# A value bank copied to SBUF, a SiLU issued two products later, four products held in their order

## The chip, the core and the metric

The kernel runs on one core of a Trainium2 chip. The metric is device time in microseconds (us) for one execution. TensorE (PE in the rows; PEld is its weight load), VectorE (DVE), ScalarE (ACT), GpSimd (POOL) and the DMA queue of SyncE (SP) each work through an instruction stream of their own in order and wait for each other by semaphores.

## The reference

One layer of a diffusion backbone over 1024 tokens of width 1024: a token mixer, and then a ConvGLU channel mixer, which is where the change lies. With `D_FF = 2816` and tokens on a grid of 16 rows by 64:

```python
p = h @ w_up_l                            # 1024 -> 2 * 2816
val, gate = p[..., :D_FF], p[..., D_FF:]
gate = depthwise_3x3(gate on the grid)    # one 3x3 filter per channel
out = (silu(gate) * val) @ w_down_l       # 2816 -> 1024
```

Everything is float32.

## The kernel before

Each float32 product is made of three matmuls on rounded high and low parts (`mm3`, lines 189 to 193: high by high, high by low, low by high). The channels of the up projection are handled in 22 blocks `f` of 128 channels. The tokens are in two groups of 512, so a block has four results: gate for group 0 and 1, value for group 0 and 1.

**Blocks 0 and 1** are made plainly. `pvs[f][0]` and `pvs[f][1]` are the gates, `pvs[f][2]` and `pvs[f][3]` the values, each 128x512 in one PSUM bank. There are eight banks of that size: two under the tag `mm`, three under `g`, one under `a`, and a pair `cv`. The loop over `d` (lines 1691 to 1702) finishes `pvs[f][1]` and `pvs[f][3]` with `up2` while the second token group is still being turned, and `sums` builds the token operands for what follows.

**Blocks 2 to 21** take seven products each in place of eight (a Strassen-Winograd scheme over the halves of the input channels and the two column groups). A product is 12 matmuls of 128x128 by 128x512. I write f.p for product p of block f; the order traced in `seq` is 2.1, 2.2, 2.5, 2.6, 2.3, 2.7, 3.1, 2.4, 3.5, 3.2, 3.6, 3.3, 3.7, 4.1, 3.4, 4.5, 4.2 and so on. They accumulate in three banks of a block: A (tag `g`) takes products 1, 6, 7 and 4, B (tag `mm`) product 2, C (tag `mm`) products 5 and 3. After products 1, 5, 6 and 7 the bank is copied to SBUF by ScalarE (line 1734), and the next product into that bank waits for the copy. A is let go by the value multiply of its own block; B and C by the writes into `pad` (lines 1741 and 1745).

**Behind the products** runs `finish(f)`: nine taps of the 3x3 filter over `pads[f % 2]` into `cv` (the first on ScalarE, line 1489, eight on VectorE, line 1491), then the SiLU of `cv` (ScalarE, line 1495), then two multiplies by the value (`mul`, VectorE, recorded at line 1468 like every sum of `tt`) and a store. `cv` is one buffer, so a block's taps start when the SiLU before is done, and `pads` are two, so the writes into the pad of block f wait for the taps of block f-2. These steps stand in a queue `back`, from which `work` takes two or three after each product.

When the products of block 2 start, `pvs[1][2]` has been copied to SBUF (`spare`, line 1576), and its `g` bank goes to A of block 2. The other two `g` banks hold `pvs[0][3]` and `pvs[1][3]`, until the second multiplies of blocks 0 and 1. A of block 3 takes the first of them, A of block 4 the second.

Pages (`pg`) are 36 SBUF buffers of 128x1024 that token operands, weights, gates and split parts share.

The framework's planner orders the instructions of each engine: it steps through the traced program with costs of its own and issues what it thinks is ready, earlier traced first. So the order on an engine is that of the plan, and where the chip is slower than the plan somewhere, an engine waits in that order. `tc.issue_after(x)` ties what is traced in its block behind `x` on the same engine, in the order of issue only.

Of the kernel before, what the change touches and what calls it, by code (L numbers as in the profile page):

```python
# [12 lines left out]
AF = mybir.ActivationFunctionType  # L13
# [5 lines left out]
P = 128  # L19
# [25 lines left out]
def grp(ap, g):  # L45

    v = ap.rearrange("p (a n) -> p a n", a=4)
    return v[:, 1:3] if g == 0 else v[:, 0::3]
# [52 lines left out]
class Kern:  # L101
# [87 lines left out]
    def mm3(self, out, ah, al, bh, bl, start, stop, **kw):  # L189
        nc = self.nc  # L190
        nc.tensor.matmul(out, ah, bh, start=start, stop=False, **kw)  # L191
        nc.tensor.matmul(out, ah, bl, start=False, stop=False, **kw)  # L192
        nc.tensor.matmul(out, al, bh, start=False, stop=stop, **kw)  # L193

    def rsqrt(self, out, ss, scale, pool):

# [1248 lines left out]
    def ffn(self):  # L1445
        nc, tc, A = self.nc, self.tc, self.A
        V = nc.vector
        wu = A["w_up"][0].rearrange("(k p) n -> p k n", p=P)
        with tc.tile_pool(name="ffn", bufs=1, reuse_waits="tile") as fp:
# [5 lines left out]
            g = [None] * NF  # L1455
# [11 lines left out]
            def tt(eng, o, a, b, op=ALU.add):  # L1467
                eng.tensor_tensor(o, a, b, op=op)  # L1468
# [3 lines left out]
            back = deque()  # L1472
            convd = set()

            def work(n):
                for _ in range(n):
                    if back:
                        back.popleft()()

            def finish(f, val):  # L1480

                c3 = self.cv.rearrange("p (r c) -> p r c", c=64)
                pad = pads[f % 2]

                def tap(k):
                    w = self.dw[:, k * NF + f:k * NF + f + 1]
                    src = pad[:, k // 3:k // 3 + 16, k % 3:k % 3 + 64]
                    if k == 0:
                        nc.scalar.mul(c3, src, w)  # L1489
                    else:  # L1490
                        V.scalar_tensor_tensor(c3, src, w, c3, op0=ALU.mult, op1=ALU.add)  # L1491

                def silu():
                    g[f] = self.pg()
                    nc.scalar.activation(g[f], self.cv, AF.Silu)

                def mul(i):
                    gt = g[f]
                    tt(V, grp(gt, i), grp(gt, i), val(i).rearrange("p (a n) -> p a n", a=2), ALU.mult)
                    if i and f < NF - 5:  # L1500
                        nc.sync.dma_start(gd[f], gt)
                        g[f] = None

                for k in range(9):
                    back.append(lambda k=k: tap(k))
                back.append(lambda: convd.add(f))
                back.append(silu)
                back.append(lambda: mul(0))
                back.append(lambda: mul(1))
# [14 lines left out]
            def to_pad(f, j, pv):  # L1524
                for rows, c in (((5, 13), 0),) if j == 0 else (((1, 5), 0), ((13, 17), 256)):
                    n = rows[1] - rows[0]
                    nc.scalar.copy(pads[f][:, rows[0]:rows[1], 1:65],
                                   pv[:, c:c + 64 * n].rearrange("p (r c) -> p r c", c=64))
# [37 lines left out]
            pvs = [[None] * 4 for _ in range(2)]  # L1566
# [8 lines left out]
                        turn(0)  # L1575
            nc.scalar.copy(self.spare, pvs[1][2])
            pvs[1][2] = self.spare

# [12 lines left out]
            def gpart(f, i):  # L1593

                if f not in here:
                    here[f] = [f >= NF - 5] * 2
                    if not here[f][0]:
                        g[f] = self.pg()
                c = slice(512 * i, 512 * i + 512)
                if not here[f][i]:  # L1600
                    nc.sync.dma_start(g[f][:, c], gd[f][:, c])
                    here[f][i] = True
                return g[f][:, c]
# [38 lines left out]
            def load(f):  # L1642
                if f >= NF or f in raws:
                    return
                raws[f] = []
                for col in (DFF + f * P, f * P):
                    if f % 2:
                        r = self.pg().rearrange("p (k n) -> p k n", k=ND)
                    else:
                        r = self.wp.tile([P, ND, P], F32, tag="raw", bufs=2, name=self.nm("wr"))  # L1650
                    nc.sync.dma_start(r, wu[:, :, col:col + P])
                    raws[f] += [flat(r[:, 0:4]), flat(r[:, 4:8])]

            def prepw(f, p, paged=False):
                a00, a01, a10, a11 = raws[f]
                S = Ss.setdefault(f, {})
                e = (V, nc.gpsimd)
                if p in (1, 2, 4):
                    src = {1: a00, 2: a01, 4: a11}[p]
                else:  # L1660
                    src = S[p] = big("s")
                    a, b = {5: (a10, a11), 6: (S.get(5), a00), 3: (a01, S.get(6)), 7: (a00, a10)}[p]
                    tt(e[(8 if f > 9 else 160) >> p & 1], src, a, b, ALU.add if p == 5 else ALU.subtract)
                if paged:
                    hl = self.page2()
                    h, l = hl[:, 0], hl[:, 1]
                else:
                    h = self.wp.tile([P, 512], F32R, tag="wh", bufs=4, name=self.nm("wh"))
                    l = self.wp.tile([P, 512], F32R, tag="wl", bufs=4, name=self.nm("wl"))
                nc.scalar.copy(h, src)  # L1670
                self.sub_l(nc.gpsimd, l, src, h)
                W[f, p] = h, l
# [11 lines left out]
            B = {1: h0[:4], 2: h0[4:], 3: h1[4:], 4: TB[3], 5: TB[0], 6: TB[1], 7: TB[2]}  # L1684
# [21 lines left out]
                    sums(d)  # L1706
            for f in range(2):
                to_pad(f, 1, pvs[f][1])
            for f in range(2):
                finish(f, lambda i, f=f: pvs[f][2 + i])  # L1710

# [2 lines left out]
            for n, (f, p) in enumerate(seq):  # L1714
                if n + WA < len(seq):
                    f2, p2 = seq[n + WA]
                    load(f2)
                    if p2 == 1:
                        load(f2 + 1)
                    prepw(f2, p2)  # L1720
                x = st.setdefault(f, {})
                bank = {2: "B", 5: "C", 3: "C"}.get(p, "A")
                if p in (1, 2, 5):
                    x[bank] = self.psum({"A": "g", "B": "mm", "C": "mm"}[bank])
                ps = x[bank]
                h, l = W.pop((f, p))
                for d in range(4):
                    c = slice(d * P, d * P + P)
                    b = B[p][d]
                    self.mm3(ps, h[:, c], l[:, c], b[:, 0], b[:, 1], start=(d == 0 and p in (1, 2, 5)), stop=(d == 3),  # L1730
                             skip_group_check=True)
                if p in (1, 5, 6, 7):
                    x[p] = big("m")
                    nc.scalar.copy(x[p], ps)
                pad = pads[f % 2]
                if p == (6 if f == 2 else 2):

                    while f - 2 not in convd:
                        work(1)
                    r = lambda t: t.rearrange("p (r c) -> p r c", c=64)  # L1740
                    tt(V, pad[:, 5:13, 1:65], r(x["B"]), r(x[1]))
                if p == 3:
                    for o, c in ((1, 0), (13, 256)):
                        r = lambda t: t[:, c:c + 256].rearrange("p (r c) -> p r c", c=64)
                        tt(V, pad[:, o:o + 4, 1:65], r(ps), r(x[6]))
                    finish(f, lambda i, x=x: (x["A"], x[5])[i])
                if p == 7:
                    tt(nc.gpsimd, x[5], x[5], x[7])
                work(2 + (len(back) > 14))
                if n >= len(seq) - 7:  # L1750
                    for _ in range(3):
                        if order:
                            gpart(order.pop(0), 0)
                if n >= len(seq) - 4:
                    i = len(ops)
                    ops[i] = prep(i)
# [49 lines left out]
            for ps in range(7):  # L1806
                bk = banks[BSET[ps]]
                for j in range(NJ):
                    n = ps * NJ + j
# [82 lines left out]
```

## Time and profile before

| what | us |
|---|---|
| three timed executions | 1362.15, 1360.96, 1357.66 |
| their median | 1360.96 |
| the profiled execution | 1357.89 |
| its span, first to last instruction | 1356.1 |

The profiled execution lies 3.07 us under the median and 1.79 us above its own span. Times in the rows are from the start of the span. The first 700 us are the mixer; products of blocks 2 to 21 run from about 733 to 1120, the down projection after that. A small share of the matmul records is missing from the trace.

### The profile page before, as it was taken

Reading aid. Unit: us, or ns where it says so; the run is one execution under the profiler, and the core shown is the slowest. Engines: PE = TensorE matmul, PEld = TensorE weight load, DVE = VectorE, ACT = ScalarE, POOL = GpSimd, SP = SyncE. Lnnn points to the kernel's source line nnn. Section 1 sums busy time; section 2 is a strip of 40 time slices with the busy share of each in tenths; the row PEclk is TensorE's granted clock in tenths of the full one; section 3 lists DMA queues with packets and bytes.
Section 4 is the critical chain, followed back from the end, with each engine's and each line's share of the span. In section 5 each row is a group of like instructions: output and inputs, shape, how many; then the busy total and the mean of one; then the engine's idle time right before and its main releaser. Section 6 shows DMA issues by size and latency. Waiting matters only on the chain.

```text
span 1356.1 us, 19253 instructions
## 1 busy us (share of the span) xinstructions
PE 1282.6 (95%) x6678; PEld 1023.2 (75%) x6678; DVE 987.9 (73%) x1750; ACT 636.5 (47%) x1324; POOL 472.2 (35%) x464
## 2 busy tenths in 40 slices
PE   5999999999899999999999899999999999999994
PEld 3777886567557789887777688888888887888883
DVE  4465555944973856757369899878888789878997
ACT  4663456532554233444757444444444444555442
POOL 0220114332434252542125667666665650000000
PEclk9999999999999999999999999999999999999997
DMA  9622226676476877815432233331233156645665
GB/s 341 196 85 72 73 84 198 210 212 210 154 202 235 270 235 273 281 61 171 171 124 79 78 93 94 94 93 60 67 93 94 47 192 235 215 127 173 200 226 187
DMA packets 183731, 213.67 MB, mean 158 GB/s; under 512 B 31639, under 2 KB 119761, under 8 KB 183633
## 3 DMA queue, kind: packets, MB, share of 16 engines
q1 hardware_dynamic: 181553, 208.19, 47.8%
q0 software_dynamic: 864, 3.15, 0.7%
q8 instruction: 53, 0.87, 0.3%
q10 hardware_dynamic: 1216, 1.09, 0.2%
q14 instruction: 45, 0.37, 0.1%
HBM read 163.11 MB, written 49.28 MB: 157 GB/s over the span
## 4 chain that ended last, share of the span: by engine, by line
PE 45%; DVE 16%; issue 5%; DMA 4%; ACT 4%; POOL 3%; SPq 0%; DVEq 0%; POOLq 0%; ACTq 0%
PE ps L191 12%; PE ps L193 11%; PE ps L192 11%; PE ps L1098 4%; DVE cv L1491 3%; PE ps L1042 2%; DVE pg L1468 1%; POOL pg L165 1%; DVE s L1468 1%; PE ps L312 1%; POOL pg L1023 1%; DVE pg L165 1%; DVE wl L165 1%; DVE pad L1632 1%; PE ps L1029 1%
## 5 line engine op out<-in xcount | busy, mean ns | idle before, releaser
L191 PE MATMUL ps<-pg,wh 128*128 128x512 f32 (+1 forms) x896 | 351.3, 393 | 7.7 <-DVE pad L1468 5.5
L193 PE MATMUL ps<-pg,wl 128*128 128x512 f32 (+1 forms) x896 | 346.5, 387 | 0.0
L192 PE MATMUL ps<-pg,wh 128*128 128x512 f32 (+1 forms) x896 | 345.9, 386 | 0.0
L1491 DVE SCALAR_TENSOR_TENSOR cv<-pad,dw,cv 128x1024 f32<-128x1024 f32 x176 | 226.3, 1286 | 12.0 <-ACT cv L1489 8.6
L191 PEld LDWEIGHTS ps<-pg,wh 128*128 128x128 f32 x896 | 169.8, 190 | 55.9 <-issue 21.0
L193 PEld LDWEIGHTS ps<-pg,wl 128*128 128x128 f32 x896 | 169.7, 189 | 35.8 <-issue 3.5
L192 PEld LDWEIGHTS ps<-pg,wh 128*128 128x128 f32 x896 | 169.9, 190 | 30.4 <-issue 0.4
L165 POOL TENSOR_TENSOR wl<-wr,wh 128x512 fp32r<-128x512 f32 x68 | 89.8, 1327 | 185.5 <-ACT wh L183 157.4
L165 POOL TENSOR_TENSOR wl<-s,wh 128x512 fp32r<-128x512 f32 x80 | 107.2, 1342 | 61.6 <-ACT wh L1670 61.3
L1670 ACT CAST wh<-s 128x512 fp32r<-128x512 f32 x80 | 49.5, 622 | 119.4 <-PE ps L192 116.5
L193 PE MATMUL ps<-wh,pg 128*128 128x512 f32 x250 | 98.1, 394 | 2.6 <-POOL pg L165 2.6
L191 PE MATMUL ps<-wh,pg 128*128 128x512 f32 x250 | 97.9, 393 | 2.2 <-ACT pg L1635 1.7
L192 PE MATMUL ps<-pg,pg 128*128 128x512 f32 (+1 forms) x248 | 96.8, 392 | 3.0 <-POOL pg L165 2.8
L191 PE MATMUL ps<-pg,pg 128*128 128x512 f32 (+1 forms) x248 | 98.1, 397 | 1.1 <-DVE pg L493 0.8
L192 PE MATMUL ps<-wl,pg 128*128 128x512 f32 x250 | 97.4, 390 | 0.0
L193 PE MATMUL ps<-pg,pg 128*128 128x512 f32 (+1 forms) x248 | 95.9, 391 | 0.8 <-POOL pg L165 0.6
L1098 PE MATMUL ps<-pg,pg 128*128 128x128 f32 x464 | 59.0, 277 | 0.9 <-ACT pg L1158 0.9
L1098 PEld LDWEIGHTS ps<-pg,pg 128*128 128x128 f32 x464 | 55.4, 192 | 3.2 <-ACT pg L1158 1.2
L192 PEld LDWEIGHTS ps<-pg,pg 128*128 128x128 f32 x248 | 47.3, 191 | 13.4 <-POOL pg L165 3.6
L193 PEld LDWEIGHTS ps<-wh,pg 128*128 128x128 f32 x250 | 47.1, 188 | 13.1 <-POOL pg L165 3.5
L191 PEld LDWEIGHTS ps<-pg,pg 128*128 128x128 f32 x248 | 47.3, 191 | 12.4 <-DVE pg L493 1.2
L193 PEld LDWEIGHTS ps<-pg,pg 128*128 128x128 f32 x248 | 46.9, 190 | 12.6 <-issue 1.7
(364 smaller groups left out, 2419.2 us busy)
## 6 DMA issues: line engine op xcount, KB each, us to landing
pg<-in_w_down_dram SPq DMA_DIRECT2D x97, 256.0 KB, 4.2
wr<-in_w_ada_dram SPq DMA_DIRECT2D x32, 512.0 KB, 4.8
wr<-in_w_up_dram SPq DMA_DIRECT2D x24, 512.0 KB, 4.1
wr<-in_w_in_dram SPq DMA_DIRECT2D x20, 512.0 KB, 3.8
pg<-in_w_up_dram SPq DMA_DIRECT2D x20, 512.0 KB, 6.5
wr<-in_w_down_dram SPq DMA_DIRECT2D x35, 256.0 KB, 2.9
gd<-pg SPq DMA_DIRECT2D x17, 512.0 KB, 2.9
pg<-gd SPq DMA_DIRECT2D x34, 256.0 KB, 4.0
```

The source lines that it names most:

```text
L165: eng.tensor_tensor(l, full, h.bitcast(F32), op=ALU.subtract)
L191: nc.tensor.matmul(out, ah, bh, start=start, stop=False, **kw)
L192: nc.tensor.matmul(out, ah, bl, start=False, stop=False, **kw)
L193: nc.tensor.matmul(out, al, bh, start=False, stop=stop, **kw)
L312: nc.tensor.matmul(ps[32 * j:32 * j + 32, :], self.csil[:, k, :], t[:, a, :], start=(k < 4), stop=(k >= 4), skip_group_check=True, tile_po ...
L1023: nc.gpsimd.tensor_tensor(dst[:, d].rearrange("p h (b c) -> p h b c", b=4), src.unsqueeze(2).broadcast_to([P, H, 4, 32]), mask, op=ALU.mult)
L1029: nc.tensor.matmul(ps[:, h * P:(h + 1) * P], Wt[:, d, h], Q[:, d, h], start=True, stop=True, skip_group_check=True)
L1042: nc.tensor.matmul(ps[po, h * n:(h + 1) * n], Q[k0:k0 + kn, d, h, po], R[k0:k0 + kn, d, h, c0:c0 + n], start=True, stop=True, skip_group_c ...
L1098: nc.tensor.matmul(ps[:, hs(h)], lhs(h), rhs(h), start=True, stop=True, skip_group_check=True)
L1468: eng.tensor_tensor(o, a, b, op=op)
L1491: V.scalar_tensor_tensor(c3, src, w, c3, op0=ALU.mult, op1=ALU.add)
L1670: nc.scalar.copy(h, src)
```

## The change

`pvs[0][3]`, a value of block 0, is copied by ScalarE to half a page as soon as it is complete, and the multiply reads the copy. Six empty steps ahead of the SiLU of block 0 in `back` have it traced after product 2.7 and its copy, two products later than before. The SiLUs of blocks 0 and 1 are tied behind the newest product copy on ScalarE. Products 6 to 9 of `seq` (3.1, 2.4, 3.5, 3.2) are each tied behind the last matmul traced before them.

```diff
@@ mm3
-        nc.tensor.matmul(out, al, bh, start=False, stop=stop, **kw)
+        self.lastmm = nc.tensor.matmul(out, al, bh, start=False, stop=stop, **kw)
@@ finish
                 def silu():
                     g[f] = self.pg()
-                    nc.scalar.activation(g[f], self.cv, AF.Silu)
+                    with tc.issue_after(self.copied.ins) if f < 2 else ExitStack():
+                        nc.scalar.activation(g[f], self.cv, AF.Silu)
...
                 back.append(lambda: convd.add(f))
+                if f == 0:
+
+                    back.extend([lambda: None] * 6)
                 back.append(silu)
@@ ffn
             pvs[1][2] = self.spare
+            spare2 = self.pg()[:, 0:512]
...
                 to_pad(f, 1, pvs[f][1])
+            nc.scalar.copy(spare2, pvs[0][3])
+            pvs[0][3] = spare2
...
-                for d in range(4):
-                    c = slice(d * P, d * P + P)
-                    b = B[p][d]
-                    self.mm3(ps, h[:, c], l[:, c], b[:, 0], b[:, 1], start=(d == 0 and p in (1, 2, 5)), stop=(d == 3),
-                             skip_group_check=True)
+                with tc.issue_after(self.lastmm.ins) if 6 <= n < 10 else ExitStack():
+                    for d in range(4):
+                        c = slice(d * P, d * P + P)
+                        b = B[p][d]
+                        self.mm3(ps, h[:, c], l[:, c], b[:, 0], b[:, 1], start=(d == 0 and p in (1, 2, 5)), stop=(d == 3),
+                                 skip_group_check=True)
                 if p in (1, 5, 6, 7):
                     x[p] = big("m")
-                    nc.scalar.copy(x[p], ps)
+                    self.copied = nc.scalar.copy(x[p], ps)
```

## Rows read from the trace of the kernel before

**Rows 1.** The head of the page.

```profile
span 1356.1 us, 19253 instructions
```

**Rows 2.** Busy time by stretch: engine busy us (instructions), granted clock, DMA share, GB/s.

```profile
750.00:757.00 7.00, 1.69 (x8) 1.07 (x6) 6.73 (x7) 1.49 (x2) 3.44 (x3) 0.99 0.26 75
...
760.00:850.00 90.00, 90.00 (x398) 74.49 (x397) 81.49 (x81) 38.83 (x61) 60.22 (x46) 1.00 0.31 93
850.00:1100.00 250.00, 249.51 (x1100) 206.04 (x1099) 204.64 (x210) 110.44 (x173) 157.87 (x119) 1.00 0.27 80
...
1150.00:1300.00 150.00, 150.00 (x664) 124.24 (x663) 132.70 (x214) 75.52 (x139) 0.00 (x0) 1.00 0.58 190
1300.00:1356.00 56.00, 37.51 (x161) 29.59 (x159) 48.57 (x120) 19.54 (x44) 0.00 (x0) 0.86 0.54 191
```

**Rows 3.** PE's waits from 700 us on: total us, times, longest us.

```profile
PE ps L191 <- DVE pad L1468: 5.5, 1, 5.5
...
PE ps L191 <- ACT pg L1635: 1.7, 1, 1.7
```

**Rows 4.** PE in order of time around the stall: start, us, instruction [idle before].

```profile
743.21 0.50 PE L191 MATMUL ps<-pg,wh 128*128 128x512 f32 x1 [1.24 <-ACT m L1734]
...
751.30 0.39 PE L193 MATMUL ps<-pg,wl 128*128 128x512 f32 x1
757.22 0.76 PE L191 MATMUL ps<-pg,wh 128*128 128x512 f32 x1 [5.54 <-DVE pad L1468]
```

**Rows 5.** VectorE in order of time, 749 to 776 us.

```profile
749.67 6.58 DVE L1491 SCALAR_TENSOR_TENSOR cv<-pad,dw,cv 128x1024 f32<-128x1024 f32 x5
756.38 1.36 DVE L1468 TENSOR_TENSOR pad<-ps,m 128x512 f32<-128x512 f32 x3
757.65 1.27 DVE L1468 TENSOR_TENSOR pg<-pg,ps 128x512 f32<-128x512 f32 x2
...
765.41 0.69 DVE L1468 TENSOR_TENSOR s<-s,wr 128x512 f32<-128x512 f32 x1 [2.63 <-POOL wl L165]
...
774.27 0.70 DVE L1468 TENSOR_TENSOR pg<-pg,spare 128x512 f32<-128x512 f32 x1 [0.30 <-ACT pg L1495]
774.89 0.67 DVE L1468 TENSOR_TENSOR pg<-pg,ps 128x512 f32<-128x512 f32 x1
```

**Rows 6.** ScalarE in order of time, 738 to 758 us.

```profile
738.36 0.62 ACT L1463 CAST pg<-m 128x512 fp32r<-128x512 f32 x1 [4.57 <-DVE m L1468]
...
740.46 1.16 ACT L1489 ACTIVATE cv<-pad,dw 128x1024 f32<-128x1024 f32 x1
...
756.28 1.02 ACT L1495 ACTIVATE pg<-cv 128x1024 f32<-128x1024 f32 x1 [5.51 <-DVE cv L1491]
757.21 0.58 ACT L1734 COPY m<-ps 128x512 f32<-128x512 f32 x1
```

**Rows 7.** Line 1576, the copy to spare: ns min/median/max.

```profile
L1576 ACT COPY spare<-ps x1: 577/577/577, 707.7 to 707.7; 128x512 f32<-128x512 f32 x1
```

**Rows 8.** Busy time by stretch after the stall (columns as rows 2).

```profile
757.20:760.50 3.30, 3.28 (x8) 2.62 (x9) 3.26 (x6) 2.14 (x4) 2.37 (x2) 0.52 0.22 82
757.20:777.80 20.60, 20.58 (x84) 16.92 (x85) 17.39 (x21) 9.28 (x15) 12.00 (x10) 0.92 0.34 101
```

**Rows 9.** PE in order of time at the end of that stretch.

```profile
777.84 0.39 PE L191 MATMUL ps<-pg,wh 128*128 128x512 f32 x1
```

**Rows 10.** PE at an earlier stall of 2.36 us.

```profile
633.27 0.50 PE L193 MATMUL ps<-wh,pg 128*128 128x512 f32 x1 [2.36 <-POOL pg L165]
```

**Rows 11.** Stretches after that stall and after the 1.7 us one (columns as rows 2).

```profile
635.00:637.00 2.00, 2.00 (x6) 1.52 (x6) 2.00 (x4) 0.00 (x0) 0.00 (x0) 0.50 0.00 0
...
1137.00:1139.00 2.00, 1.81 (x8) 1.50 (x9) 2.00 (x4) 1.70 (x4) 0.00 (x0) 1.00 0.95 336
```

**Rows 12.** SyncE's queue, the loads of block 3's weights.

```profile
726.74 4.08 SPq L1651 DMA_DIRECT2D pg<-in_w_up_dram  x2
```

**Rows 13.** VectorE in order of time, late in the up products.

```profile
1100.15 0.76 DVE L1468 TENSOR_TENSOR pad<-ps,m 128x256 f32<-128x256 f32 x2 [2.08 <-PE ps L193]
```

## The prediction

> **What bounds the kernel now.** I read the page first, then the busy time by stretch. The span is 1356.1 us [rows 1]. From 760 to 850 and from 1150 to 1300 PE is busy for the whole stretch, and from 850 to 1100 for 249.51 of 250 us [rows 2]. Little can be won there: 250 us hold 1100 matmuls, 0.227 us each, so a product of 12 takes 2.72 us and seven of them, a block's worth, take 19.05 us. VectorE is busy 204.64 of the same 250 us, so it has about a fifth of its time spare and can catch up when it is late. Only at two places behind 740 us does PE stand out as idle: from 750 to 757, where it is busy 1.69 of 7 us, and in the last 56 us.
>
> Next I read PE's waits from 700 us on. One wait of 5.5 us, for a VectorE write into `pad`, is worth more than all the others together [rows 3]. PE in order of time shows its place: the last matmul before starts at 751.30, the next at 757.22 [rows 4]. Counting 12 matmuls to a product, the one that ends there is 2.7.
>
> Then I read the other engines over the same stretch, to see why nothing could run. The released instruction waits for the first `pad` write, 756.38 to about 757.06, and that write stands behind the last five taps of block 0 [rows 5]. It lets bank B of block 2 go, so the waiting product is 3.5, which the plan has put ahead of 3.1 and 2.4. Why not those? 3.1 needs a `g` bank, and the first to come free is that of `pvs[0][3]`, after the second multiply of block 0, at 758.92 (757.65 + 1.27) [rows 5]. 2.4 needs the copy of 2.7, which is done on PE by 751.7, but ScalarE issues it behind the SiLU, which itself waits for the taps until 756.28; the copy starts at 757.21 [rows 6]. So three products wait for one tap chain by three different ways.
>
> **What the stall costs.** Without it 3.1 would start at 751.53 (751.30 + 0.23). That leaves 5.69 us to 757.22. After it the granted clock is 0.52, the lower of its two levels (1.2 of 2.4 GHz), until 760.5, and 8 matmuls take 3.30 us [rows 8] where 8 x 0.227 = 1.82 us would do: some 1.5 us more. As a check, from 757.20 to 777.80 there are 84 matmuls, seven products [rows 8], and the next product, 4.1, starts at 777.84 [rows 9]. Without a stall it would start at 751.53 + 19.05 = 770.58. The whole prize is therefore 7.26 us.
>
> **The change part by part.** *The bank.* With `pvs[0][3]` in SBUF its bank is free long before 751, and 3.1 can follow 2.7 at once. *The SiLU.* With the copy of 2.7 ahead of it on ScalarE, that copy runs at about 751.8 and 2.4 can follow 3.1 at 754.3. The SiLU still cannot start before the taps are done, at 756.28, so it loses nothing unless more is put ahead of it. Its page, its multiplies and the store of the gate move with it, and so do the weight loads behind that store in SyncE's queue; the multiplies stay where they were in time, so these do too. *The order.* The four ties make PE take 3.1, 2.4, 3.5, 3.2 in turn. 3.1 and 2.4 fill 5.44 us, up to 756.97, and 3.5 then finds B free at 757.06. A tie is an order of issue and no instruction; I cost it at nothing, and its risk is only that PE holds back something ready behind something that is not.
>
> *The copy* is one more instruction on ScalarE, 0.58 us by the copy to `spare` [rows 7]. Where the plan puts it decides what it costs. Below: ScalarE stands idle for 4.57 us ahead of 738.36, and the value is complete by then, so nothing. Above: it goes with the gate copies that come after that cast, just ahead of the first tap at 740.46 [rows 6]; then the whole tap chain is late by 0.55 us. It is traced with the gate copies, so I take the upper end. 3.5 then starts at 757.06 + 0.55 + 0.16 (the hand-off from write to matmul that the trace shows now) = 757.8. The pause of 1.24 us ahead of 743.21, for a product copy behind that tap [rows 4], grows as much, but 3.5 waits for B all the same, so it isn't counted again.
>
> A multiply from `spare` takes 0.70 us against 0.67 from a bank [rows 5], so the multiply gains nothing from its new source. The Trainium skill (VectorE: DVE Perf Modes, Rules for kernel authors) advises to copy PSUM to SBUF first only if many operations follow, and one follows here; by that rule the copy is a plain loss of its 0.58 us and the sum is 1361.5. That is rival D below. What the rule leaves out is the bank.
>
> *The page.* The second load of block 3's weights is issued by 730.82 (726.74 + 4.08), held for a page [rows 12]. With one page fewer it may slip by a few us. Its first reader on PE is 3.5, now after 757, so 26 us cover it; I cost it at nothing.
>
> **What is late next.** Banks again. 4.1 needs a third `g` bank. A of block 3 sits in that of `pvs[0][3]`, A of block 2 is busy, and the last holds `pvs[1][3]`, freed by the second multiply of block 1, which ends at 775.56 (774.89 + 0.67) [rows 5]. In the kernel before this is 2.3 us ahead of 4.1; now PE gets there sooner. PE: 3.5 at 757.8 and five products, 13.6 us, give 771.4. VectorE: the chain of block 1 begins as before, as it needs the SiLU of block 0. It loses its pause of 2.63 us ahead of 765.41, spent waiting for GpSimd, which waits for weight buffers that PE lets go [rows 5]; they are let go some 7 us sooner now. So the multiply ends at 775.56 - 2.63 + 0.55 = 773.48, and 4.1 starts at 773.64. PE stands for 2.2 us, and the lead that is left is 777.84 - 773.64 = **4.2 us**.
>
> Does a stall of 2.2 us lower the clock? One of 1.7 us [rows 3] left it at 1.00; one of 2.36 us [rows 10] was followed by a stretch at 0.50 [rows 11], about seven matmuls at 0.2 us more, 1.4 us. But that one had other pauses close before it, and here PE is dense for 20 us. I take nothing, and keep 1.4 us for the range.
>
> Later banks have slack: the next of this kind, 5.1, comes 19 us after 4.1 and waits for a multiply of block 2 that VectorE reaches some 15 us after that of block 1. From there PE is the bound and the lead is kept, since VectorE's chains start on PE's results: late in the stage it still waits 2.08 us for PE [rows 13]. The down projection and the tail then move forward whole.
>
> **The sum.** 7.26 - 0.55 - 0.3 (3.5 ready a little before B) - 2.2 = 4.2 us. The span goes from 1356.1 to 1351.9, the profiled execution from 1357.89 to 1353.7; from the median, 1360.96, it is **1356.8 us**. The runs shown spread over 4.5 us, so a difference under 0.3%, 4.1 us, cannot be told from no change here.
>
> **The rivals.**
> - *A, the forecast.* 4.1 waits for block 1's second multiply. Gain 3.2 to 5.2 us. Chance 0.46.
> - *B, no second stall.* The plan puts 3.4, whose bank needs no VectorE, ahead of 4.1, as it put 3.5 ahead of 3.1 before. Then 3.4 starts at 771.4, 4.1 after it, and the lead is 777.84 - 771.4 = 6.4 us: 1354.6. For it: the planner does swap products. Against: in the plan the taps were done sooner than on the chip, or it would not have put the SiLU ahead of 2.7's copy, so it may see no wait at 4.1. Chance 0.22.
> - *C, a larger second stall.* VectorE's order keeps its 2.63 us pause, 4.1 starts at 776.3 and 1.6 us are left (1359.4); or the clock falls, 4.2 - 1.4 = 2.8 us (1358.2). Work later than the empty steps is also traced up to three steps further back for some blocks, and where PE has no idle time a new order can only lose. Chance 0.16.
> - *D, the copy buys nothing.* Something else holds 3.1, for instance its bank still going to another product in the plan, and the copy's 0.58 us is all that is left: 1361.5. Against: the weights of 3.1 are split before the stall, and the tie names 3.1 first. Chance 0.08.
> - *E, slower: the SiLU goes too far back.* Its tie is to the newest copy traced; the plan may set further ScalarE work ahead of it, up to copies that wait for PE. 4.1 starts 16.8 us after the SiLU (773.64 against 756.83). It is back at 777.84 when the SiLU starts at 761.0, which is behind the copy of 3.5. Behind that of 3.6 (766.5) it would start 9.7 us late: 5.5 us slower, 1366.5. Against: in the plan the SiLU is ready early. Chance 0.08.
>
> **The numbers.** Gains over 4.1 us are B and six tenths of A: 0.50. Within are the rest of A, C and most of D: 0.42. Slower is E: 0.08. The range runs from B less 2 us of scatter of the median, 1352.5, to D, 1361.5; E and the fringes of B and D stay out, about 0.2.
>
> **What the new profile would show.** If right: no PE gap over 1 us at 751 to 757 and a clock of 1.00 behind it; one `g` bank copy of 0.58 us on ScalarE before 742; the copy of 2.7 ahead of the first SiLU and that SiLU still near 757; 3.1 and 2.4 unbroken before 3.5; a PE wait of about 2 us near 771, ended by a VectorE multiply (line numbers move by a few); and from there the same rows about 4 us earlier down to the end. No wait at 771 and a lead over 6 us is B. A wait over 4 us there, or a slow clock behind it, is C. The old gap still there is D. A SiLU after 761 is E. I am also wrong if the lead is there at 800 and gone at 1150, by a gap like that at 1137 grown longer, or if the plan orders the down projection's tail in another way: the last 56 us hold 18 us of PE idle time [rows 2] that no step of mine touches.

## The result, and the profile after

The change makes the kernel slower. The median is 1369.76 us (five runs, 1367.63 to 1375.27) against 1360.96 us; the ratio is 1.0068, 95% interval 1.0044 to 1.0092. The forecast was 1356.8 us, range 1352.5 to 1361.5. The profiled execution of the changed kernel took 1369.26 us.

The stretches of the changed kernel, with the columns of [rows 2]:

```profile
span 1367.5 us, 19250 instructions
...
750.00:757.00 7.00, 7.00 (x31) 5.78 (x32) 3.40 (x3) 2.93 (x6) 4.72 (x4) 1.00 0.01 2
...
780.00:790.00 10.00, 8.94 (x28) 6.84 (x28) 6.94 (x10) 4.18 (x7) 5.05 (x4) 0.68 0.33 107
790.00:847.00 57.00, 54.03 (x238) 44.22 (x236) 50.33 (x52) 24.34 (x38) 34.82 (x27) 1.00 0.24 74
847.00:852.00 5.00, 4.76 (x14) 3.77 (x15) 4.54 (x5) 2.00 (x5) 3.79 (x3) 0.66 0.91 253
850.00:1100.00 250.00, 249.74 (x1099) 206.38 (x1098) 204.65 (x210) 108.89 (x170) 156.70 (x119) 1.00 0.27 80
1150.00:1300.00 150.00, 149.78 (x661) 123.59 (x660) 130.15 (x210) 76.91 (x142) 0.00 (x0) 1.00 0.55 180
```

From 750 to 757, where PE was busy for 1.69 of 7 us [rows 2], it is now busy throughout: the stall that the change aims at is gone. But two stretches of low clock stand where 760 to 850 was full before. PE in order of time shows why:

```profile
749.99 0.50 PE L191 MATMUL ps<-pg,wh 128*128 128x512 f32 x1 [1.44 <-ACT m L1742]
...
780.34 0.77 PE L191 MATMUL ps<-pg,wh 128*128 128x512 f32 x1 [4.11 <-DVE pad L1468]
781.83 0.80 PE L191 MATMUL ps<-pg,wh 128*128 128x512 f32 x1 [0.72 <-DVE pg L1468]
...
847.24 0.50 PE L191 MATMUL ps<-pg,wh 128*128 128x512 f32 x1 [3.21 <-ACT m L1742]
```

The first line is 2.3, waiting for the copy of 2.5; the kernel before has no wait there. The second is one matmul of 4.5, which the plan put ahead of 4.1, waiting for a write into `pad` that stands behind the last tap of block 1; the third is 4.1, waiting for block 1's second multiply. The fourth is 6.4, counted 23 products on: it needs the copy of 6.7. ScalarE in order of time shows where these copies stood, and the rows of the first blocks:

```profile
748.83 0.62 ACT L1675 CAST wh<-pg 128x512 fp32r<-128x512 f32 x1 [2.84 <-DMA pg<-in_w_up_dram]
749.36 0.58 ACT L1742 COPY m<-ps 128x512 f32<-128x512 f32 x1
...
756.14 0.58 ACT L1742 COPY m<-ps 128x512 f32<-128x512 f32 x1
...
761.05 1.02 ACT L1496 ACTIVATE pg<-cv 128x1024 f32<-128x1024 f32 x1 [3.03 <-DVE cv L1491]
...
844.50 1.02 ACT L1496 ACTIVATE pg<-cv 128x1024 f32<-128x1024 f32 x1 [5.42 <-DVE cv L1491]
845.55 1.12 ACT L1489 ACTIVATE cv<-pad,dw 128x1024 f32<-128x1024 f32 x1
846.61 0.58 ACT L1742 COPY m<-ps 128x512 f32<-128x512 f32 x1
```

The copy of 2.7 (756.14) is ahead of the first SiLU, as intended. But at 844.50 block 5's SiLU waits 5.42 us for its taps, and the copy of 6.7 stands behind it and behind a first tap: the old stall's pattern, five blocks later. And at 748.83 a cast waits for a transfer that nothing waited for before, and the copy of 2.5 (749.36) stands behind it. SyncE's queue, whose loads of block 3 stood at 726.74 [rows 12], shows that transfer:

```profile
743.05 0.38 SPq L1656 DMA_DIRECT2D wr<-in_w_up_dram  x1
743.52 1.55 SPq L1656 DMA_DIRECT2D pg<-in_w_up_dram  x2
758.34 0.37 SPq L1656 DMA_DIRECT2D wr<-in_w_up_dram  x1
```

Block 3's two loads now come behind the first load of block 4. GpSimd and VectorE wait for them, each in its own row:

```profile
752.28 1.28 POOL L1468 TENSOR_TENSOR s<-pg 128x512 f32<-128x512 f32 x1 [4.66 <-DMA pg<-in_w_up_dram]
```

```profile
753.60 1.77 DVE L1468 TENSOR_TENSOR s<-s,pg 128x512 f32<-128x512 f32 x1 [3.85 <-POOL s L1468]
...
763.01 1.28 DVE L1468 TENSOR_TENSOR pg<-pg,pg 128x512 f32<-128x512 f32 x1
...
767.99 1.78 DVE L1468 TENSOR_TENSOR s<-s,wr 128x512 f32<-128x512 f32 x1 [2.50 <-POOL wl L165]
```

The sum at 753.60 stands among the taps of block 0. They end at 761.01, 2.4 us later than before once the start of the stage is lined up.

**Lined up.** To see where time goes I took the same matmul, counted from the last one, in each trace, less the time of the last transpose before the up products (722.62 us before, 725.00 after), so that scatter of the stages ahead drops out. The table gives the difference to the kernel before, in us, from one profile of each kernel; the columns are the end of block 0's taps and the matmuls that stood at 771, 798, 880 and 1318 us before. The last column is the measured ratio to the kernel before.

```
kernel                 taps 0   771    798    880    1318   ratio
after                  +2.38  -4.17  +3.64  +8.41  +8.67   1.0068
e1 own tile            -0.01  -7.00  -1.99  +2.73  +3.01   1.0022
e2 page, copy only     +2.17  +1.07  +1.07  +1.08  +1.18   1.0015
e3 own, copy only      -0.01  -1.02  -1.02  -1.02  -1.03   1.0008
e4 steps, no copy      +3.76  +5.86  +5.86 +11.60 +11.84   1.0068
e5 catch up            +0.01  -6.95  -1.81  +2.90  +3.02   1.0005
e6 + 3.4 first         -0.01  -6.97  -0.01  +1.16  +1.03   1.0010
e7 three taps less     -0.03  -7.02  -3.13  -0.96  -1.75   0.9979
e8 loads first         -0.06  -7.04  -1.95  +2.77  +2.74   1.0013
e9 + sums on GpSimd    -3.45  -7.29  -6.86  -5.44  -4.57   0.9959
e10 + 3.4 first        -3.45  -7.32  -5.98  -3.75  -3.57   0.9956
e11 sums, before       -4.05  -3.95  -3.95  +2.45  +3.23   1.0003
e12 e9 without steps   -3.47  -5.43  -5.43  -3.87  -3.66   0.9963
```

For the changed kernel: 4.2 us won at the first stall, 7.8 lost at the second, 4.8 at the third (8.41 - 3.64), and the rest runs along. That is +8.7 us, the measured difference of the medians (8.8).

### The profile page after: what moved, and what is told of

Read it like the earlier page. It is cut to its first block, busy times and chain, and to the rows that moved or that the text cites. A ratio compares the mean times of both kernels' runs of the same rounds, so it can differ in the third digit from the quotient of the medians.

```text
span 1367.5 us, 19250 instructions
## 1 busy us (share of the span) xinstructions
PE 1285.0 (94%) x6678; PEld 1022.3 (75%) x6678; DVE 986.5 (72%) x1750; ACT 635.9 (47%) x1325; POOL 469.0 (34%) x464
## 4 chain that ended last, share of the span: by engine, by line
PE 44%; DVE 15%; issue 7%; POOL 4%; DMA 4%; ACT 3%; SPq 0%; DVEq 0%; POOLq 0%; ACTq 0%
PE ps L191 12%; PE ps L192 11%; PE ps L193 11%; PE ps L1098 3%; DVE cv L1491 3%; PE ps L1042 2%; POOL pg L165 1%; POOL wl L165 1%; DVE pg L165 1%; DVE pg L1468 1%; DVE s L1468 1%; DVE wl L165 1%; PE ps L312 1%; POOL pg L1023 1%; DVE pad L1637 1%
```

## The experiments

The theory after this reading was: the page taken for the copy pushes block 3's loads back, and all the rest follows. The rival was that the six empty steps make the new stalls whatever the page. The ties of the four products need no run in the changed kernel: with and without them the instructions stand in the same order on every engine. The SiLU's tie changes nothing without the steps. With the steps it does: without it the plan puts block 0's SiLU ahead of the copy of 2.7 again. So three parts act, the copy, its page and the steps, and "the steps" means the steps with that tie; no run parts the two.

**e1, own tile.**

```
-        self.idb = cp.tile([P, H, P], BF16, name="idb")
+        self.spare2 = cp.tile([P, D // 2], F32, name="spare2")
+        self.idb = self.spare2.bitcast(BF16)[:, :H * P].rearrange("p (h n) -> p h n", h=H)
...
-            spare2 = self.pg()[:, 0:512]
+            spare2 = self.spare2
```

> The changed kernel, with the value of 2.7's bank copied into a tile of its own (room freed by laying it over a mixer table that is no longer read) and not into one of the 36 pages; six empty steps and ties stay. Theory 'page' (the page taken for the copy pushes block 3's two weight loads on SyncE behind block 4's first one, and all that hangs on them is late): the loads go back in front, the first taps end about 2.5 us sooner after the pad write, the stalls at 780 and 847 us of the changed kernel shrink below 2 us in all, and the time is 1355 to 1360 us. Rival 'empty steps' (the later SiLU and the reshuffled order make the stalls, whatever the page): the stalls of 4.1 and 3.2 us stay and the time is 1366 to 1370 us.

Ratio 1.0022, interval 1.0002 to 1.0043. The loads go back in front and the taps end as before (-0.01), so by the table the page is about two thirds of the loss (8.67 against 3.01). But both later stalls stay; PE in order of time:

```profile
777.79 0.47 PE L191 MATMUL ps<-pg,wh 128*128 128x512 f32 x1 [2.09 <-DVE pad L1469]
779.28 0.79 PE L191 MATMUL ps<-pg,wh 128*128 128x512 f32 x1 [1.02 <-DVE pg L1469]
```

The first stall now gives the full 7.0 us, the second takes 5.0 of them and the third 4.7. Neither theory alone: the ratio makes 1364 us of the 1360.96, which lies between the two ranges.

**e2, the copy into a page alone; e3, the copy into its own tile alone.** Both drop the steps and the ties:

```
-                if f == 0:
-                    back.extend([lambda: None] * 6)
```

> The copy into a page alone, without the six empty steps and without the ties. Theory 'page': block 3's loads still come after block 4's, so most of the loss stays: 1364 to 1369 us. Rival 'empty steps': the product 4.5 is no longer split with one matmul ahead of 3.4, the first SiLU is back where it was, and the time is 1354 to 1359 us.

> The copy into the tile of its own, without the six empty steps and ties: neither suspect is there, only the bank's early release. Both theories: no stall of 5.5 us at 757 and none over 2 us behind it, 1353 to 1359 us. If it is at or above 1362 us, the release of the bank itself costs what the forecast did not count, and both theories fall.

Ratios 1.0015 (0.9995 to 1.0035) and 1.0008 (0.9989 to 1.0026). By these ratios e2 is at 1363 us and e3 at 1362 us, between the ranges expected for e2 and above the one for e3; e3's interval (1359.5 to 1364.5 us) does not decide whether it reaches the 1362 at which both theories were to fall. Without the steps the late stalls are gone (the table's rows are flat after 771), but the first stall is not won either: in e3 it only moved. ScalarE in e3:

```profile
759.31 1.02 ACT L1497 ACTIVATE pg<-cv 128x1024 f32<-128x1024 f32 x1 [6.05 <-DVE cv L1492]
760.23 0.58 ACT L1740 COPY m<-ps 128x512 f32<-128x512 f32 x1
```

The copy at 760.23 is that of 2.7, behind the waiting SiLU; PE has done 3.1 and then stands 3.97 us for it ahead of 2.4. The Trainium skill (TensorE: Matmul & The Clock Gate, Architectural detail) says that ScalarE works its queue strictly in order; the trace agrees, 6.05 us long. My expectation that no stall over 2 us would be left was wrong. e2 against e3 also shows the page alone: its taps end 2.2 us later, and the same matmul comes 2.1 us later.

**e4, the steps without the copy.**

> The six empty steps and the ties alone; the value of 2.7 stays in its bank, no page is taken. Theory 'page': the loads stand as before, and the time stays within 3 us of 1361 us, with a stall near 757 us still there unless the order alone removes it. Rival 'empty steps': the SiLU of block 0 comes two products later and the loss of about 9 us shows here too, 1366 us or more.

Ratio 1.0068 (1.0045 to 1.0091), the loss that the rival named, but not by its way. One of PE's waits and one row of VectorE in this kernel:

```profile
PE ps L191 <- DVE pg L1468: 11.2, 1, 11.2
```

```profile
748.06 5.54 DVE L1468 TENSOR_TENSOR s<-s,pg 128x512 f32<-128x512 f32 x1 [1.94 <-POOL s L1468]
```

With the value still in its bank, 3.1 waits 11.2 us for the multiply that frees it. The multiply waits for the SiLU, and the SiLU for the taps, which end 3.8 us later by the table: the sum shown, which stands among them, took 5.54 us here and 1.77 us in the kernel before. So this run is not the steps alone. Of the 5.9 us lost up to 771 some 3.8 are that sum's, an estimate that lets PE follow the taps one for one. And here the products' ties do act: without them the plan starts 3.5 and puts 2.4 ahead of 3.1. What the steps would do alone is not shown. Shown is that the copy alone only moves the stall (e3), that the steps with the ties, without the copy, do harm (e4), and that copy and steps together take it away (e1).

**e5, catch up.** After the first SiLU the queue is emptied faster:

```
-                work(2 + (len(back) > 14))
+                work(2 + (len(back) > 14) + (3 if n in (6, 7) else 0))
```

> As e1 (own tile, six empty steps, ties), but three steps more are taken from the queue after each of the products 3.1 and 2.4, so that from the second block's SiLU on every step is issued at the product at which the kernel before issues it. Theory 'left over' (the six empty steps stay in the queue as a lag behind the first SiLU, put later SiLUs ahead of product copies on ScalarE, and so make the stall of 3.2 us at 844): that stall is gone, the one near 778 stays as in e1 (2.1 and 1.0 us), and the time is some 4.4 us below e1. Rival 'chain' (VectorE's chain is late there whatever the order): both stalls stay and the time is that of e1.

Ratio 1.0005 (0.9985 to 1.0025), and in the table the row of e1 over again: the third stall is still 3.2 us. The lag that the steps leave in the queue is not its cause.

**e6, 3.4 ahead of 4.1.**

```
-                    seq += [(f, 1), (f - 1, 4)] + [(f, p) for p in (5, 2, 6, 3, 7)]
+                    seq += ([(f - 1, 4), (f, 1)] if f == 4 else [(f, 1), (f - 1, 4)]) + [(f, p) for p in (5, 2, 6, 3, 7)]
...
-                with tc.issue_after(self.lastmm.ins) if 6 <= n < 10 else ExitStack():
+                with tc.issue_after(self.lastmm.ins) if 6 <= n < 17 else ExitStack():
```

> As e5, with 3.4 put ahead of 4.1 and the ties carried on over the products up to 5.1, so that TensorE has 2.7 us of ready work while 4.1 and 4.5 wait for VectorE. Theory 'chain' for the second stall (TensorE runs 7 us ahead and then waits for block 1's taps and product): the wait before 4.1 shrinks from 3.1 us to under 1 us and the time is 2 to 4 us below e5, about 5 to 7 us below the kernel before. Rival 'order alone': if what costs time there is something other than that wait, no difference to e5 above 1 us.

Ratio 1.0010 (0.9989 to 1.0030): no gain. ScalarE in e6:

```profile
773.02 1.02 ACT L1497 ACTIVATE pg<-cv 128x1024 f32<-128x1024 f32 x1 [3.38 <-DVE cv L1492]
774.07 1.12 ACT L1490 ACTIVATE cv<-pad,dw 128x1024 f32<-128x1024 f32 x1
...
775.64 0.57 ACT L1743 COPY m<-ps 128x512 f32<-128x512 f32 x1
```

Now 3.4 is the one that waits (4.40 us), for the copy of 3.7 behind block 1's SiLU. Whatever the product order, PE meets the same thing: the taps of block 1 end when they end.

**e7, three taps less.**

```
-                    else:
+                    elif not (f == 1 and k > 5):
```

> As e1, but three of the eight VectorE taps of block 1 are left out, so the values of that block are not those of the reference; VectorE has 3 x 1.32 = 4.0 us less to do ahead of block 1's SiLU. Theory 'chain': the second stall (2.1 and 1.0 us at 778, with 5.0 us lost in all there) goes to nothing, and the third shrinks with it by up to 3 us, so the time is 5 to 8 us below e1. Rival 'steps' (the order makes the stalls): the second stall stays, less than 1.5 us gained.

Ratio 0.9979 (0.9958 to 1.0000), 5.9 us below e1 by the two ratios and 4.8 by the table. With 4 us less on VectorE 3.9 us are lost at the second stall (-7.02 to -3.13) where e1 lost 5.0, and 2.2 where e1 lost 4.7. VectorE's chain sets both stalls. But the second did not go to nothing, as I had expected: it is one wait of 1.98 us now (772.55), for a copy that stands behind block 1's SiLU as in e6, with a low clock behind it (0.52 from 772.5 to 776).

**e8, loads first.** The page stays; only the order in which the two are asked for is turned:

```
-            spare2 = self.pg()[:, 0:512]
...
             load(2)
+            load(3)
+            spare2 = self.pg()[:, 0:512]
```

> The changed kernel, its page kept, but block 3's two weight loads are issued before that page is taken. Theory 'page' (the page costs time only by pushing these loads behind block 4's): the time falls from the changed kernel's 1.0068 times that of before to e1's 1.002, 5 to 6 us, and the casts and sums of block 3 wait no longer for a transfer. Rival 'one page fewer' (the pool of 35 is short further on as well): the time stays above 1.005 times that of before.

Ratio 1.0013 (0.9995 to 1.0031). SyncE's queue:

```profile
702.52 2.02 SPq L1655 DMA_DIRECT2D pg<-in_w_up_dram  x2
740.36 10.45 SPq L1655 DMA_DIRECT2D wr<-in_w_up_dram  x2
```

The kernel has one page fewer, as the changed one, and behaves as e1: the loads stand at 702.52, well ahead of block 4's at 740.36. The page costs time only through the place of these loads.

**What holds VectorE.** In e1 and e8 the chain's pace is set by more than taps. VectorE in e1:

```profile
799.88 3.93 DVE L1492 SCALAR_TENSOR_TENSOR cv<-pad,dw,cv 128x1024 f32<-128x1024 f32 x3
807.14 1.79 DVE L1469 TENSOR_TENSOR s<-s,wr 128x512 f32<-128x512 f32 x1 [3.32 <-POOL wl L165]
```

A weight sum for a later product stands among the taps and waits for GpSimd. In e9 and e10 the sums of products 6 and 3 of blocks 3 to 5 go to GpSimd; e11 does that alone to the kernel before, e12 is e9 without the steps:

```
-                    tt(e[(8 if f > 9 else 160) >> p & 1], src, a, b, ALU.add if p == 5 else ALU.subtract)
+                    tt(e[(8 if f > 9 else 232 if 2 < f < 6 else 160) >> p & 1], src, a, b, ALU.add if p == 5 else ALU.subtract)
```

> As e8 (page kept, block 3's loads ahead of it, six empty steps and ties), and the weight sums for the products 6 and 3 of blocks 3 to 5 go from VectorE, where each stands in the row of taps and waits there for GpSimd (2.3 us before one sum, 3.3 us before another in e1), to GpSimd. Theory 'loop' (after the bank is free, TensorE runs into VectorE's chain, which itself waits in its row for sums whose buffers TensorE and GpSimd free late): the pauses of 2.3 and 3.3 us in VectorE's row go, the third stall (3.2 us, 4.4 lost) goes, the second (5.0 lost) shrinks by 2 to 3 us; 6 to 8 us below e8, which puts it 4 to 6 us below the kernel before. Rival 'taps alone' (the taps themselves set VectorE's pace and the pauses fall in slack): less than 2 us below e8.

> As e9, with 3.4 ahead of 4.1 and the ties carried on over the products up to 5.1. Theory 'loop': TensorE has 2.7 us of ready work at the second stall and no late sums behind it; equal to e9 or up to 2.5 us below it. Rival 'copy behind SiLU' (as in e6, where the stall of 4.4 us moved to the next product, whose copy stood behind block 1's SiLU on ScalarE): no gain over e9, a stall of about 4 us with ScalarE's copy as its end near 776.

> The kernel before, unchanged but for the same move of the sums of blocks 3 to 5 to GpSimd. If the stall at 757 us sets the pace there, and not VectorE's pauses behind it, then this is worth nothing: within 2 us of the kernel before, the stall of 5.5 us still there. If it gains 4 us or more, e9's gain is the move's own and says nothing of the change.

> As e9 without the six empty steps, so that block 0's SiLU stands on ScalarE ahead of the copy of 3.1 again. Theory 'the later SiLU is needed' (in e3 the freed bank alone bought nothing because that copy stood behind the SiLU): a stall of 3.5 to 5 us near 762 us that ScalarE's copy ends, and a time 3 to 6 us above e9, about that of the kernel before. Rival 'the steps only cost' (the lag they leave in the queue outweighs the copy's place): equal to e9 or below it.

e9: 0.9959 (0.9945 to 0.9974), e10: 0.9956 (0.9939 to 0.9972), some 6 us below the kernel before: both beat both kernels, as expected, and putting 3.4 first adds nothing that can be told. VectorE in e9, and the stretch that was at 0.68 in the changed kernel:

```profile
745.32 10.55 DVE L1491 SCALAR_TENSOR_TENSOR cv<-pad,dw,cv 128x1024 f32<-128x1024 f32 x8
...
759.59 10.56 DVE L1491 SCALAR_TENSOR_TENSOR cv<-pad,dw,cv 128x1024 f32<-128x1024 f32 x8 [0.21 <-ACT cv L1489]
```

```profile
775.00:790.00 15.00, 15.00 (x68) 12.42 (x67) 14.20 (x13) 6.50 (x10) 14.77 (x12) 1.00 0.27 96
```

The eight taps of blocks 0 and 1 run in one piece each. Block 0's end 3.45 us sooner; of 7.3 us won at the first stall 0.4 are lost at the second and 1.4 at the third.

e11: 1.0003 (0.9985 to 1.0022). By itself it is worth nothing that can be told, but not as expected: the 5.5 us stall shrank to 2.2, and 6.4 us were lost again between 798 and 880. e12: 0.9963 (0.9949 to 0.9978), not to be told from e9, where 3 to 6 us more were expected. Its expectation names the copy of 3.1; by the tiles it is that of 2.7. It does stand behind the SiLU again, but the taps end so early that PE stands only 1.56 us for it: once the taps run in one piece the six steps buy nothing. What e12 has and e11 lacks is the copy and block 3's loads asked for early; no run has those loads early without the copy, so which of the two earns the difference is not shown. By the table 1.5 us of it come up to 771 and 4.9 between 798 and 880.

## Why the prediction was wrong

**Right.** The whole prize of 7.26 us: e1 and e8 win 7.0 at that place. The bank, the order 3.1, 2.4, 3.5, 3.2 and the copy of 2.7 ahead of the SiLU came as described. One reading of the rows was wrong, without weight for the sum: PE's other waits from 700 us on add up to 6.0 us, so the one of 5.5 us is not worth more than all of them together. The copy's 0.55 us was an upper end: in e8 the first tap starts 0.5 us later, and the taps still end 0.06 us sooner, since the pauses among them take it up.

**The step that failed: the page.** "With one page fewer it may slip by a few us. Its first reader on PE is 3.5, now after 757, so 26 us cover it; I cost it at nothing." The loads slipped by 14.4 us (743.52 - 726.74 less the 2.38 of the line-up). The cover was counted to PE. The readers that came first were a cast on ScalarE and a sum on GpSimd, and behind that sum one of VectorE's among the taps, which wait in their rows with everything behind them. On ScalarE the copy of 2.5 stood behind the cast, and PE waited 1.44 us for it (749.99), the largest part of the 2.8 us that are missing at the first stall (4.2 against 7.0). On VectorE the taps came 2.4 us later, and the second stall took 2.8 us more (7.8 against 5.0). Together that is some 5.7 us by e1, 7.5 by the ratios of the changed kernel and e8.

**Mis-sized: the second stall.** The mechanism was right (4.1 waits for block 1's second multiply, with one matmul of 4.5 put in front that waits for the same chain), at 2.2 us and no clock. Without the page it took 5.0 us (e1), with it 7.8. I let VectorE's pause of 2.63 us go whole, and put the multiply 2.1 us sooner. In the changed kernel the pause was 2.50 us. In e1 it was 0.43, but the sum behind it took 1.78 us in place of 0.69, and the taps ended only 1.0 us sooner. The granted clock, which I left out, was 0.68 from 780 to 790, the two levels mixed.

**Also failed: "From there PE is the bound and the lead is kept".** 6.4 waited 3.2 us behind block 5's SiLU and the place lost 4.7 us. VectorE does have a fifth of its time spare later, but it was still behind there, held by sums that wait for GpSimd. e5 excludes the lag left by the steps; e7 and e9 show VectorE's chain. Why the first stall's pattern returns at this block and not at another (in e11 it comes at 820 and 856) stays open.

Together: the forecast was 4.2 us won and 8.7 were lost, 12.9 us apart. By the table the page is 5.7 of them, the second stall 2.8 (5.0 in e1 against 2.2), the third 4.7; the first stall gave 0.6 us more than the sum had (7.0 against 6.4), and the last 0.3 came further on.

**The rivals.** C came nearest in mechanism, with its pause and its clock, but at 1359; its price lacked the loads and the third stall. E (1366.5) was the only rival that was slower, and its sign, a SiLU after 761, was there: 761.05, or 758.67 with the 2.38 us of the line-up taken off. That the time fell on its side is luck: the SiLU waited there 3.03 us for taps that the loads had made late, and no product copy was put ahead of it beyond that of 2.7. D's rule, that of the Trainium skill (VectorE: DVE Perf Modes, Rules for kernel authors), by which the copy is a plain loss, gave 1361.5. e3 tries the copy alone: 1.0008, no difference that the interval allows to be told, so neither the rule's loss nor a gain is seen; with the chain relieved, e12 (0.9963) against e11 (1.0003), the copy and early loads gain together, and the part of the copy is not shown.

## What to carry to other kernels

A buffer taken from a shared pool can move the transfers that ask the pool after it: look who reads that transfer first on every engine, not only on the one that is the bound, and ask for the transfer first. A stall removed on the bounding engine is worth what the next engine's chain leaves of it; before freeing a bank, see what waits inside that chain, in order, for others. Here the loads asked for first, and six small sums moved to an engine with room (worth nothing that could be told alone), turned a loss of 9 us into a gain of 6.

## What the runs showed of the hardware

A multiply whose value comes from SBUF takes as long as one from a bank only when GpSimd is quiet. At 763.01 in the changed kernel it took 1.28 us beside a GpSimd sum (762.45 to 763.74), against 0.68 for the multiply from a bank at 762.42; the sums at 753.60 and 767.99 took 1.77 and 1.78 us where the one at 765.41 in the kernel before took 0.69 [rows 5]. The Trainium skill (SBUF — State Buffer, SBUF: two separate sides) has the rule: a VectorE instruction with two SBUF inputs and a GpSimd one that reads SBUF exclude each other for a whole instruction. The trace agrees, with 0.6 to 1.1 us each here. In e4 the price was 4.9 us: the sum at 748.06 took 5.54 us while GpSimd ran four instructions without a pause up to 753.05, and ended 0.55 us after the last of them. The forecast's 0.70 us came from one multiply (774.27) beside which GpSimd stood idle from 774.42 on.

A wait of 3.2 us behind a full stretch was enough for a low clock (0.66 from 847 to 852). Behind e1's waits of 2.09 and 1.02 us, with one matmul between, matmuls took 0.43 us in place of 0.23; behind one of 1.26 us in e9 the clock stayed at 1.00. The length of a wait alone does not decide: behind 1.98 us in e7 the clock was 0.52 (772.5 to 776), behind 2.17 us in e11 it was 1.00 (757 to 761).

The kernel before, run with the experiments, had medians of 1361.99 to 1364.87 us, and the stretch behind the matmul at 1318 us took 19.4 to 24.6 us in the profiles, though none of these edits touches its code. So each ratio is taken against runs on the same chip, and single profiles are read up to 1318 us only.
